# Four accumulating loads emitted earlier, and the fourth token sums split between VectorE and GpSimd

## The chip, the cores and the metric

The kernel runs on one core of one Trainium2 chip. The metric is the device time of one execution in microseconds (us). The core has five engines that run side by side, each with its own queue that it works through in order: TensorE (PE in the profile), which multiplies matrices into PSUM; VectorE (DVE) and ScalarE (ACT), which read PSUM and SBUF; GpSimd (POOL), which works on SBUF; and SyncE (SP), which only issues transfers. ScalarE and GpSimd issue some transfers as well. The data moves on 16 DMA engines that all these queues share.

## The reference

One encoder block over 1024 tokens of 1024 features, in float32. Cut to what matters:

```python
h = rms_norm(x, norm1_g)
a, gate, q, k, v = split(h @ w_in)          # 512 columns each
conv_out = conformer_conv(a, gate, ...)      # GLU, 31-tap depthwise convolution, LayerNorm, silu
attn_out = neighbourhood_attention(rms_norm(q), rms_norm(k), v, rpb)
mix = concatenate([conv_out, attn_out])      # 1024 tokens x 1024
x = x + mix @ w_out                          # output projection and residual
h = rms_norm(x, norm2_g)
x = x + (silu(h @ w_gate) * (h @ w_up)) @ w_down   # 2816 hidden features
```

The change touches two places: the residual sum `x + mix @ w_out`, and the preparation of `h` for the gate and up products.

## The kernel before

Every product of float32 matrices is made of three matmuls. An operand is split into a high part (`fp32r`, a cast by ScalarE) and the remainder (a subtraction on VectorE or GpSimd); `split` emits both, and `mac` emits the three matmuls (lines 122 to 124, 128x512 each). The cast always comes first, and the remainder waits for it.

The output projection, the gate and up products and the down product are each done as two by two blocks in seven block products in place of eight, which need sums and differences of blocks beforehand.

**The output projection** is the products n1, n7, n4, n6, n5, n2, n3, in this order. `group` (line 1112) runs one: for each of four token blocks `cb`, in the order 0, 3, 1, 2, it emits four macs and then `read`, which adds the result from PSUM into the token tiles `x2` on VectorE (`put`, line 865). n7 goes on in the PSUM of n1, and n5 in that of n6, so these reads combine two products. The `x2` tiles 0 to 3 are loaded with the rows of `x`; tiles 4 to 7 are written by the reads of n1, and the rows of `x` are added to them by a transfer that accumulates. `add_x(t)` (line 861) issues it from GpSimd's queue, 512 KB each. The reads of n5 add to tiles 0 to 3 and 4 to 7, those of n2 and n3 to 4 to 7 alone. After the last read of a tile `norm2` stores it to DRAM through SP and takes its sum of squares on ScalarE.

**What sets the order** is written out by hand. `weaves(n, s0=..., s1=...)` lays a row of n steps, and after each mac `weave()` takes one step off it: the step's instructions go into their engines' queues at that place of the program. An engine reaches them when it has done what stands before them. `take` loads and splits the next weight half (ScalarE casts, GpSimd subtracts); `QS` splits a left operand with GpSimd; `C` and `U` are transposes on TensorE with their copies on ScalarE; `N` is a normalisation on VectorE and `lo2` a remainder on VectorE. The weights' raw tiles have three buffers (`R`), so SP's next load waits until GpSimd has split an older one.

**The gate and up products.** `products` lists them: product 0 to 7 are m1 and m2 of four feature blocks, then come, in pairs of blocks 0 and 1, m6 (products 8 and 9), m5 (10 and 11), m7 (12 and 13), m3 (14 and 15) and m4 (16 and 17), and so on. Each has four macs. m6 and m5 of a block share a PSUM bank, as do m7 and m4: m5 can start only when VectorE has evacuated m6 (`u2`, line 1185). After each product `evac` takes the result out, and `prep` splits the weights of the product that comes four later (tiles `t0m`, `t1m`, ...; cast on ScalarE, remainder on GpSimd).

The left operands are sums of token blocks. `s_sum(t, 3)` makes the third sum S3 of token tile t (line 1037, into the first half of `xT`), `s_sum(t, 4)` the fourth, S4 (line 1033): two instructions of 128x256, which read `xT[t]` and `sn[t]` and write into two tiles `s4` that are taken when the first of them is emitted. `SP(name, t)` splits a sum with ScalarE and VectorE. m7 needs all four splits of S3, m3 those of S4, and m4 those of A22. A split of S4 needs the fourth sums of all four tokens. `plan` lays these steps beside the products by number: `8: dict(s1=SP("S3", 2), ...)` is emitted during product 8.

Nearly all tiles of 128x1024 come from one tag, `G`, with 22 buffers. When none is free, the first instruction that writes a new tile waits on its own engine until the last user of an older tile is done.

Of the kernel before, what the change touches and what calls it, by code (L numbers as in the profile page):

```python
# [74 lines left out]
def build(ctx, tc, a):  # L75
    nc = tc.nc
    pe, act, dve, pool = nc.tensor, nc.scalar, nc.vector, nc.gpsimd
# [560 lines left out]
    def score_mm(i):  # L638
        s_, hp = divmod(i, 4)
        rh, cb = order[s_]  # L640
        t = rh * 4 + cb
        c0, ncol, _ = WIN[cb]
        out = []
        for hh in range(2):
            s = mm(f"s{i}{hh}")[:, :AR * ncol]
            pe.matmul(s, qT[hh * HD:(hh + 1) * HD, hp, t * P:(t + 1) * P],  # L646
                      k4[hh * HD:(hh + 1) * HD, hp, rh * 4:rh * 4 + AR, c0:c0 + ncol], start=True, stop=True)
            out.append(s)
        return out
# [46 lines left out]
    rowf, diff, a11 = [], [], {}  # L696
# [45 lines left out]
    s0 = score_mm(0)  # L742
# [4 lines left out]
    s1 = score_mm(1)  # L747
# [29 lines left out]
    def q_split(n, f, j, eng):  # L777
        if j == 0:
            qop[n] = H(n, F32R)
        split(*[qop[n][:, o + j * 1024:o + j * 1024 + 1024] for o in (0, 2048)],  # L780
              f[j].rearrange("p c b q -> p (c b q)"), (eng,))
# [44 lines left out]
    def conv_silu(h, c):  # L826
        y = four(f"z{h}{c}")
        for i in range(4):
            pe.transpose(y[:, i * P:(i + 1) * P], xh[4 * h + i][:, c * P:(c + 1) * P], ident)
        act.activation(y, y, AF.Silu, bias=lnb[:, c:c + 1], scale=lng[:, c:c + 1])  # L830
        n = ("A22", "A12")[h]
        if c == 0:
            qop[n] = H(n, F32R)
        tiles = lambda w: w.rearrange("p (b i j) -> p i b j", b=4, j=16)
        hi, lo = [tiles(qop[n][:, o + c * 512:o + c * 512 + 512]) for o in (0, 2048)]
        y4 = y.rearrange("p (i b j) -> p i b j", b=4, j=16)
        split(hi, lo, y4, (dve,))
        if h == c == 0:
            tails.append(lambda: conv_diff(h, c, y4))
        else:  # L840
            conv_diff(h, c, y4)
# [10 lines left out]
    def rows(ap, t):  # L852
        rh, cb = divmod(t, 4)
        return ap.rearrange("(h i w) d -> h i w d", h=2, w=GW)[rh, :, cb * 16:cb * 16 + 16, :]
# [5 lines left out]
    def add_x(t):  # L860
        return lambda: pool.dma_start(x2[t], rows(a["x"], t), accum_op=OP.add)
# [88 lines left out]
    def norm2_out(t):  # L950
        r = SM(f"r2{t}r", 1)
        dve.reciprocal(r, sd2[t])
        xn[t] = G(f"xn{t}")
        dve.scalar_tensor_tensor(xn[t], x2[t], r, g2b, OP.mult, OP.mult)
# [68 lines left out]
    def s_sum(t, ns, eng):  # L1023
        (x11, x12), (x21, x22) = lr(xT[t]), lr(xT[t + 4])
        for n in ns:
            if n == 1:
                sn[t] = G(f"sn{t}")
            s1, s2 = lr(sn[t])
            if n == 4:
                if not s4:  # L1030
                    s4.extend(G(f"s4{j}").rearrange("p (k s) -> p k s", s=512) for j in range(2))
                for j in range(2):
                    eng.tensor_tensor(s4[j][:, :, t * P:(t + 1) * P], *[w[:, j * 256:(j + 1) * 256].rearrange(
                        "p (k s) -> p k s", s=P) for w in (x12, s2)], OP.subtract)
                continue
            o, l, r = ((s1, x21, x22), (s2, x11, s1), (x21, x11, x21))[n - 1]
            eng.tensor_tensor(o, l, r, OP.subtract)

    s4 = []
# [21 lines left out]
    def turn(t, j):  # L1061
        if not h2:
            h2.extend(H(f"h2{w}", F32R).rearrange("p (k s) -> p k s", s=512) for w in range(2))
        pt = (tp, mm)[j](f"t2{t}{j}")
        for i in range(4):
            kb = 4 * j + i
            pe.transpose(pt[:, i * P:(i + 1) * P], xn[t][:, kb * P:(kb + 1) * P], ident)
        if j == 0:
            xT[t] = G(f"xT{t}")
        w = lr(xT[t])[j]  # L1070
        if t < 4:
            hi, lo = [q[:, 4 * j:4 * j + 4, t * P:(t + 1) * P] for q in h2]
            p3 = pt.rearrange("p (k s) -> p k s", s=P)
            act.copy(hi, p3)
            act.copy(w, pt)
            rest.append(lambda: dve.tensor_tensor(lo, p3, hi.bitcast(F32), OP.subtract))
        else:
            act.copy(w, pt)
# [7 lines left out]
    def weaves(n, **at):  # L1086
        row = [[] for _ in range(n)]
        for k, fs in at.items():
            row[int(k[1:])].extend(fs if isinstance(fs, (list, tuple)) else [fs])
        woven.extend(lambda fs=fs: [f() for f in fs] for fs in row)  # L1090

    def QS(n, f, j, eng):
        return lambda: q_split(n, f, j, eng)

    def C(h, c):
        return lambda: conv_silu(h, c)

    def N(t):
        return lambda: norm2_out(t)

    def U(t, j):
        return lambda: turn(t, j)

    def SS(t, *ns, eng=dve):
        return lambda: s_sum(t, ns, eng)

    def SP(n, t, eng=dve):
        return lambda: s_split(n, t, eng)

    lo2 = lambda: rest.pop(0)()  # L1110

    def group(p, cbs=CB):
        for cb in cbs:
            more = p in ("n7", "n5")
            if not more:
                pb[cb] = mm(f"{p}{cb}")
            proj(p, cb, pb[cb], start=not more)
            read(p, cb)

    for cb in CB:  # L1120
        load_x2(cb)
    weaves(12, s0=lambda: (weigh(31), evac_hi(7), evac_lo(7)), s1=QS("Q3", diff, 0, pool), s2=lambda: tails.pop()(), s3=[lambda: read("n1", 0), add],
           s4=QS("Q3", diff, 1, pool), s6=C(0, 1), s10=take)
    group("n1", CB[1:])
    weaves(16, s1=C(0, 2), s5=take, s9=C(0, 3), s13=QS("Q2", diff, 0, pool))
    group("n7")
    weaves(16, s0=C(1, 0), s2=QS("Q2", diff, 1, pool), s4=take, s6=C(1, 1), s9=take, s12=QS("Q1", rowf, 0, pool))
    group("n4")
    weaves(16, s0=C(1, 2), s2=take, s5=C(1, 3), s7=QS("Q1", rowf, 1, pool), s10=take, s13=QS("Q4", diff, 0, pool))
    group("n6")  # L1130
    weaves(16, s1=take, s3=QS("Q4", diff, 1, pool), s6=take, s8=add_x(4), s9=N(0), s12=add_x(7), s13=N(3), s15=add_x(5))
    group("n5")
    while pos[0] < len(chunks):
        issue()
    for _ in range(3):
        next_raw()
    weaves(16, s0=take, s1=[N(1), U(0, 0)], s2=U(0, 1), s3=[lo2, lo2], s4=[U(3, 0), add_x(6)], s5=[U(3, 1), N(2)], s6=[lo2, lo2],
           s7=U(1, 0), s8=U(1, 1), s9=[lo2, lo2, prep], s10=[U(2, 0), take], s11=U(2, 1), s12=[lo2, lo2], s13=prep)
    group("n2")
    weaves(16, s3=prep, s7=prep, s9=N(4), s12=U(4, 0), s13=[U(4, 1), N(7)], s15=SS(0, 1, 2))  # L1140
# [7 lines left out]
        4: dict(s0=SP("S2", 2), s1=SP("S1", 0), s3=SP("S1", 3)),  # L1148
        5: dict(s0=SP("S1", 1), s1=SP("S1", 2), s2=SS(0, 3), s3=SS(3, 3)),
        6: dict(s0=SS(1, 3), s1=SS(2, 3), s3=SP("S3", 0)),  # L1150
        7: dict(s1=SP("S3", 3), s3=SP("S3", 1)),
        8: dict(s1=SP("S3", 2), s2=SS(0, 4, eng=pool)),
        9: dict(s0=SS(3, 4, eng=pool), s2=SS(1, 4, eng=pool)),
        10: dict(s0=SS(2, 4, eng=pool)),
        11: dict(s1=SP("S4", 0), s3=SP("S4", 1)),
        12: dict(s1=SP("S4", 2), s3=SP("S4", 3)),
        13: dict(s2=SP("A22", 0), s3=SP("A22", 1)),
# [243 lines left out]
```

## Time and profile before

| what | value |
|---|---|
| runs of the kernel, median of 3 (lowest to highest) | 1058.2 us (1057.29 to 1059.95) |
| the profiled execution's own time | 1060.61 us |
| span from its first to its last instruction | 1058.9 us |
| granted TensorE clock, mean over the span | 0.996 |
| TensorE matmuls, busy | 1033.3 us, 98% |
| VectorE, ScalarE, GpSimd busy | 68%, 44%, 43% |
| moved by DMA | 162.93 MB, 154 GB/s on the mean |

In the profile a row of the timeline gives start, duration, engine, line, operation, output and inputs, and how many instructions it merges; in brackets stand the idle time just before it and what ended it. Line 118 is the remainder and line 114 the cast of any split, so these are told apart by their tiles: `wB` is a half of B21 or B22, `wP` one of P1 to P4, `S` a token sum. `PE n` are the projection's products, `PE A`, `B` and `D` the PSUM banks of the gate and up products. A row of the stages gives the stretch, its length, each engine's busy time, the granted TensorE clock, the DMA engines' busy share and GB/s.

### The profile page before, as it was taken

The page shows a single profiled execution, that of the slowest core. Times are in us where ns is not written, and L with a number is a line of the kernel's source. Part 1 is how long each engine was busy: PE and PEld are TensorE (multiplying, and loading weights), DVE is VectorE, ACT ScalarE, POOL GpSimd, SP SyncE. Part 2 cuts the span into 40 slices and gives each one's busy share as a digit, 9 for nine tenths or more (in the row PEclk, how much of TensorE's full clock was granted, in tenths as well). Part 3 has the DMA queues.
Part 4 walks back from the last instruction along what each step waited for, and adds up shares of the span by engine and source line. Part 5 has one row for each costly group of instructions (what it writes and reads, how often), then busy time and mean ns, then how long its engine had stood idle before and what let it go on. Part 6 is the DMA issues. An engine that isn't in the chain of part 4 may idle for free.

```text
span 1058.9 us, 13907 instructions
## 1 busy us (share of the span) xinstructions
PE 1033.3 (98%) x4972; PEld 836.4 (79%) x4972; DVE 721.1 (68%) x1093; ACT 465.4 (44%) x915; POOL 455.8 (43%) x346
## 2 busy tenths in 40 slices
PE   7999999999999998999999999999999999999997
PEld 6888888776658877778888888888888888888885
DVE  6768999966895464867564564655646567758883
ACT  6455346627776556642323323232232444433441
POOL 0236668923575753675554445544455200002310
PEclk9999999999999999999999999999999999999999
DMA  9595872285545285355322233232231597633641
GB/s 337 180 260 196 236 241 78 70 238 172 151 107 163 83 213 161 100 140 183 125 100 90 110 113 112 75 129 100 83 136 73 192 328 264 208 100 121 216 132 40
DMA packets 74677, 162.93 MB, mean 154 GB/s; under 512 B 13488, under 2 KB 22192, under 8 KB 73904
## 3 DMA queue, kind: packets, MB, share of 16 engines
q1 hardware_dynamic: 67776, 144.14, 39.8%
q0 software_dynamic: 4864, 10.49, 5.9%
q10 hardware_dynamic: 1968, 7.42, 2.1%
q8 instruction: 39, 0.64, 0.2%
q14 instruction: 30, 0.25, 0.1%
HBM read 122.86 MB, written 53.15 MB: 166 GB/s over the span
## 4 chain that ended last, share of the span: by engine, by line
PE 55%; DVE 1%; issue 0%; POOL 0%; ACT 0%; DVEq 0%
PE B L123 5%; PE B L122 5%; PE B L124 5%; PE D L123 4%; PE D L124 4%; PE D L122 4%; PE A L123 3%; PE A L122 3%; PE A L124 3%; PE B2d L122 1%; PE B2d L123 1%; PE B2d L124 1%; PE A3d L122 1%; PE A2d L122 1%; PE A1d L122 1%; PE A0d L122 1%
## 5 line engine op out<-in xcount | busy, mean ns | idle before, releaser
L347 DVE SCALAR_TENSOR_TENSOR cv<-u,par,cv 128x1009 f32<-128x1009 f32 (+14 forms) x85 | 108.5, 1276 | 1.9
L373 POOL TENSOR_TENSOR pa<-pa,pr 128x1022 f32<-128x1022 f32 (+10 forms) x31 | 75.2, 2427 | 32.2 <-ACT pr L372 31.4
L1356 POOL TENSOR_TENSOR ou<-ou,resm 128x512 f32<-128x512 f32 x8 | 12.4, 1545 | 142.4 <-DMA resm<-xd 141.8
L114 ACT CAST op<-sr 128x512 fp32r<-128x512 f32 x77 | 47.6, 619 | 52.1 <-PE B2d L124 22.2
L118 DVE TENSOR_TENSOR op<-sr,op 128x512 fp32r<-128x512 f32 x77 | 59.2, 769 | 14.7 <-ACT op L114 14.7
L1193 DVE TENSOR_TENSOR g<-B,g 128x512 f32<-128x512 f32 x22 | 15.2, 690 | 74.0 <-PE B L124 74.0
L1202 ACT ACTIVATE D<-D 128x512 f32<-128x512 f32 x22 | 12.8, 582 | 113.3 <-DVE D L1201 113.3
L1185 DVE TENSOR_TENSOR u<-B,g 128x512 f32<-128x512 f32 x22 | 15.1, 690 | 61.1 <-PE B L124 61.1
L668 POOL TENSOR_SCALAR e<-e,rs 128x288 f32<-128x288 f32 (+1 forms) x64 | 34.9, 567 | 45.6 <-DVE rs L666 41.0
L114 ACT CAST op<-wd 128x512 fp32r<-128x512 f32 x66 | 40.9, 620 | 31.0 <-DVE wd L1280 17.1
L118 DVE TENSOR_TENSOR op<-wd,op 128x512 fp32r<-128x512 f32 x66 | 50.4, 764 | 2.6 <-ACT op L114 1.1
L986 DVE TENSOR_TENSOR ts<-ts,gu 128x512 f32<-128x512 f32 x36 | 43.3, 1202 | 0.6
L1191 ACT ACTIVATE A<-A 128x512 f32<-128x512 f32 x18 | 10.5, 582 | 68.6 <-PE A L124 68.6
L661 ACT ACTIVATE e<-e,mx 128x288 f32<-128x288 f32 (+1 forms) x64 | 36.2, 569 | 3.0 <-DVE mx L659 3.0
L865 DVE TENSOR_TENSOR x<-x,n 128x512 f32<-128x512 f32 x32 | 21.0, 681 | 22.7 <-PE n L124 14.3
L659 DVE CUSTOM_DVE_ANT_0 e<-s,tab 128x288 f32<-128x288 f32 (+1 forms) x64 | 29.7, 500 | 8.7 <-PE s L646 8.4
L372 ACT ACTIVATE pr<-u,par 128x1022 f32<-128x1022 f32 (+10 forms) x31 | 34.2, 1135 | 1.2 <-ACT vs L433 1.2
L677 PEld LDWEIGHTS p<-ident,e 128*96 128x96 f32 (+1 forms) x192 | 20.0, 133 | 18.0 <-POOL e L668 10.4
L677 PE MATMUL p<-ident,e 128*96 128x128 f32 (+1 forms) x192 | 28.5, 281 | 2.3 <-DVE pT L682 1.0
L986 DVE TENSOR_TENSOR ts<-gu 128x512 f32<-128x512 f32 x18 | 30.1, 1670 | 0.0
L693 PE MATMUL o<-pT,vw 96*64 96x128 f32 (+1 forms) x384 | 28.0, 281 | 0.0
L646 PE MATMUL s<-kT,qT 64*128 64x288 f32 (+1 forms) x128 | 26.7, 495 | 0.0
(1065 smaller groups left out, 3525.9 us busy)
## 6 DMA issues: line engine op xcount, KB each, us to landing
sr<-sd SPq DMA_DIRECT2D x77, 256.0 KB
gu<-in_gu SPq DMA_DIRECT2D x36, 512.0 KB
sd<-sd SPq DMA_DIRECT2D x22, 512.0 KB
wd<-in_wd SPq DMA_DIRECT2D x44, 256.0 KB
sd<-g SPq DMA_DIRECT2D x33, 256.0 KB
x<-in_x SPq DMA_DIRECT2D x12, 512.0 KB
xd<-x SPq DMA_DIRECT2D x8, 512.0 KB
resm<-xd SPq DMA_DIRECT2D x16, 256.0 KB
```

The source lines that it names most:

```text
L114: act.copy(hi, src)
L118: eng.tensor_tensor(*[w[..., sl] for w in (lo, src, hi.bitcast(F32))], OP.subtract)
L122: pe.matmul(acc, lh, rh, start=start, stop=False, skip_group_check=True)
L123: pe.matmul(acc, lh, rl, start=False, stop=False, skip_group_check=True)
L124: pe.matmul(acc, ll, rh, start=False, stop=stop, skip_group_check=True)
L347: dve.scalar_tensor_tensor(acc[:, o], uc[:, i], dwk[:, c, t:t + 1], acc[:, o], OP.mult, OP.add)
L372: act.activation(pr[:, o], uc[:, i], AF.Copy, scale=dwk[:, c, t:t + 1])
L373: pool.tensor_tensor(pa[:, o], pa[:, o], pr[:, o], OP.add)
L661: act.activation(e[:, hh], e[:, hh], AF.Exp, bias=mx, scale=-1.0, accum_out=rs[:, hh:hh + 1])
L668: pool.tensor_scalar(es[i][:, hh], es[i][:, hh], rs[:, hh:hh + 1], 1.0, op0=OP.mult, op1=OP.mult)
L677: pe.transpose(pt[:m, g * P:(g + 1) * P], es[i][:, hh, g * m:(g + 1) * m], ident)
L986: dve.tensor_tensor(lr(tsum[i, 1])[n - 3] if o is None else o, l, r, OP.add)
```

## The change

Four steps `add_x` are taken out of the rows of n5 and n2 and put into those of n7, n4 and n6. Token tiles 4 to 7 thus receive the rows of `x` before the reads of n5 add to them; before the change they received them between the reads of n5 and those of n2.

In `plan`, the fourth sums of tokens 0 and 3 stay on GpSimd and move one product earlier; those of tokens 1 and 2 go to VectorE, into products 9 and 10. The splits of S3 for tokens 1 and 2 move from products 7 and 8 to 9 and 10, in front of those sums.

```diff
     group("n1", CB[1:])
-    weaves(16, s1=C(0, 2), s5=take, s9=C(0, 3), s13=QS("Q2", diff, 0, pool))
+    weaves(16, s1=C(0, 2), s5=take, s9=C(0, 3), s11=add_x(4), s13=QS("Q2", diff, 0, pool))
     group("n7")
-    weaves(16, s0=C(1, 0), s2=QS("Q2", diff, 1, pool), s4=take, s6=C(1, 1), s9=take, s12=QS("Q1", rowf, 0, pool))
+    weaves(16, s0=C(1, 0), s1=add_x(7), s2=QS("Q2", diff, 1, pool), s4=take, s6=C(1, 1), s8=add_x(5), s9=take, s12=QS("Q1", rowf, 0, pool))
     group("n4")
-    weaves(16, s0=C(1, 2), s2=take, s5=C(1, 3), s7=QS("Q1", rowf, 1, pool), s10=take, s13=QS("Q4", diff, 0, pool))
+    weaves(16, s0=C(1, 2), s1=add_x(6), s2=take, s5=C(1, 3), s7=QS("Q1", rowf, 1, pool), s10=take, s13=QS("Q4", diff, 0, pool))
     group("n6")
-    weaves(16, s1=take, s3=QS("Q4", diff, 1, pool), s6=take, s8=add_x(4), s9=N(0), s12=add_x(7), s13=N(3), s15=add_x(5))
+    weaves(16, s1=take, s3=QS("Q4", diff, 1, pool), s6=take, s9=N(0), s13=N(3))
     group("n5")
...
-    weaves(16, s0=take, s1=[N(1), U(0, 0)], s2=U(0, 1), s3=[lo2, lo2], s4=[U(3, 0), add_x(6)], s5=[U(3, 1), N(2)], s6=[lo2, lo2],
+    weaves(16, s0=take, s1=[N(1), U(0, 0)], s2=U(0, 1), s3=[lo2, lo2], s4=U(3, 0), s5=[U(3, 1), N(2)], s6=[lo2, lo2],
            s7=U(1, 0), s8=U(1, 1), s9=[lo2, lo2, prep], s10=[U(2, 0), take], s11=U(2, 1), s12=[lo2, lo2], s13=prep)
     group("n2")
...
         6: dict(s0=SS(1, 3), s1=SS(2, 3), s3=SP("S3", 0)),
-        7: dict(s1=SP("S3", 3), s3=SP("S3", 1)),
-        8: dict(s1=SP("S3", 2), s2=SS(0, 4, eng=pool)),
-        9: dict(s0=SS(3, 4, eng=pool), s2=SS(1, 4, eng=pool)),
-        10: dict(s0=SS(2, 4, eng=pool)),
+        7: dict(s1=SP("S3", 3), s2=SS(0, 4, eng=pool)),
+        8: dict(s2=SS(3, 4, eng=pool)),
+        9: dict(s1=SP("S3", 1), s3=SS(1, 4)),
+        10: dict(s1=SP("S3", 2), s3=SS(2, 4)),
         11: dict(s1=SP("S4", 0), s3=SP("S4", 1)),
```

## The prediction

> **What bounds the kernel now.** I read the page first: TensorE (PE) is busy for 98% of the span, so the edit can only give back time that PE loses. I then asked for PE's waits.
>
> ```profile
> PE 1033.3 (98%) x4972; PEld 836.4 (79%) x4972; DVE 721.1 (68%) x1093; ACT 465.4 (44%) x915; POOL 455.8 (43%) x346
> ```
> ```profile
> PE t L1067 <- DVE x L865: 2.6, 1, 2.6
> ...
> PE B L123 <- DVE S L118: 1.5, 2, 0.7
> ...
> PE n L122 <- ACT wB L114: 0.8, 1, 0.8
> ```
>
> Of the list (engine, what it waited for, us in total, times, longest), these three are a read of the projection, a token split and a weight cast. Apart from one at the start, all the long waits lie between 388 and 463 us, in the code that the diff touches. PE's timeline shows what each costs, halved clock included.
>
> ```profile
> 379.61 0.39 PE L122 MATMUL n<-wB,A 128*128 128x512 f32 x1
> 380.29 0.39 PE L122 MATMUL n<-wB,A 128*128 128x512 f32 x1
> ...
> 381.33 0.48 PE L122 MATMUL n<-wB,A 128*128 128x512 f32 x1
> ...
> 382.46 0.48 PE L122 MATMUL n<-wB,A 128*128 128x512 f32 x1
> ...
> 390.75 1.12 PE L1067 MATMUL t<-ident,xn 128*128 128x128 f32 x4 [2.56 <-DVE x L865]
> ...
> 398.47 0.39 PE L122 MATMUL n<-wB,Q 128*128 128x512 f32 x1
> ...
> 403.26 0.50 PE L123 MATMUL n<-wB,Q 128*128 128x512 f32 x1 [1.95 <-POOL wB L118]
> ...
> 415.25 0.39 PE L122 MATMUL A<-h,t0m 128*128 128x512 f32 x1
> ```
>
> A mac (three matmuls) is 0.68 us, 379.61 to 380.29; a mac with a transpose group is 1.13, 381.33 to 382.46, so a group is 0.45. Product n2 has 16 macs and 8 groups: 10.9 + 3.6 = 14.5, but took 398.47 - 379.61 = 18.9. Stall A costs **4.4**. Product n3 has 16 macs and 2 groups, 11.8, but took 415.25 - 398.47 = 16.8. Stall B costs **5.0**. More than half of each is idling; most of the rest is a halved clock just after it:
>
> ```profile
> 392.00:394.00 2.00, 2.00 (x6) 1.52 (x5) 1.29 (x3) 0.98 (x2) 0.00 (x0) 0.50 1.04 270
> ```
>
> Further on, in the gate and up products:
>
> ```profile
> 440.13 0.39 PE L122 MATMUL B<-S,t0m 128*128 128x512 f32 x1
> ...
> 447.12 0.47 PE L122 MATMUL B<-S,t0m 128*128 128x512 f32 x1 [1.39 <-DVE u L1185]
> ...
> 458.11 0.39 PE L122 MATMUL B<-S,t0m 128*128 128x512 f32 x1
> ...
> 463.13 0.39 PE L122 MATMUL B<-S,t1m 128*128 128x512 f32 x1
> ...
> 469.28 0.39 PE L122 MATMUL D<-A,t1m 128*128 128x512 f32 x1
> ```
>
> These rows start products 8, 10, 14, 15 and 17, each of four macs, 2.72. Product 10 is 6.99 - 5.44 = **1.55** late (stall C); 14 takes 5.02 and 15 with 16 takes 6.15, so 2.3 + 0.7 = **3.0** more (stall D). All four together are 13.9 us.
>
> **Part 1, the four adding transfers.** What stalls A and B hang on:
>
> ```profile
> 390.01 0.69 DVE L865 TENSOR_TENSOR x<-x,n 128x512 f32<-128x512 f32 x1 [3.51 <-DMA x<-in_x]
> ```
> ```profile
> 381.83 3.37 SPq L977 DMA_DIRECT2D gu0None<-in_gu  x1
> ```
> ```profile
> 398.23 0.62 ACT L114 CAST t0m<-gu0None 128x512 fp32r<-128x512 f32 x1 [5.25 <-DMA gu0None<-in_gu]
> ```
> ```profile
> 379.65 2.99 POOL L861 DMA_DIRECT2D x<-in_x  x3
> ```
> ```profile
> DMA to landing us min/median/max: 10.3/15.1/18.9
> ```
> ```profile
> 350.00:355.00 5.00, 5.00 (x25) 4.14 (x25) 2.52 (x4) 3.23 (x4) 5.00 (x3) 1.00 0.08 24
> 355.00:360.00 5.00, 5.00 (x26) 4.13 (x25) 1.13 (x3) 1.77 (x3) 3.23 (x2) 1.00 0.54 186
> ...
> 375.00:380.00 5.00, 5.00 (x24) 4.14 (x23) 4.93 (x8) 3.86 (x8) 5.00 (x3) 1.00 1.01 339
> ...
> 385.00:390.00 5.00, 3.19 (x19) 2.33 (x16) 1.27 (x2) 3.69 (x8) 2.21 (x2) 1.00 1.03 207
> ```
>
> Stall A: the read of n2 into token tile 4 waits until 390.01 for its add, issued after 379.65. That read frees the PSUM bank that the next transposes want. Moved to n7, n4 and n6, the adds are issued some 20 to 35 us sooner, where the DMA engines are 8 to 54% busy; even the longest landing, 18.9, is in time. The read then follows VectorE's program order and ends near 387.1, before PE wants the bank at 388.0. **A goes: -4.4** (bounds 0 and -4.4).
>
> Stall B: ScalarE sits 5.25 us on the first gate weights; behind that cast, in its order, stands the cast of the last half of B22, and GpSimd's split of it ends at 403.26. From 398.23 that is 5.0 us. Unstalled, n3 begins at 394.1 and wants this half 1.6 later, so the weights must land by 390.7. With the adds' 2.1 MB gone, the last store (0.5 MB) and the weights (0.5 MB) need 1.5 us each at the 339 GB/s at which the stores went alone: near 386 if SP's issue is no longer held for 3.37, 398.2 if the adds are not what holds it. I take the former, as the rate falls from 339 to 207 with the adds. **B goes: -5.0** (bounds 0 and -5.0).
>
> What it costs: each issue holds GpSimd about 1.0 us (2.99 for 3). GpSimd's queue where they go, and SP's:
>
> ```profile
> 348.75 2.40 POOL L118 TENSOR_TENSOR Q<-df,Q 128x1024 fp32r<-128x1024 f32 x1 [2.82 <-ACT Q L114]
> ...
> 353.48 2.40 POOL L118 TENSOR_TENSOR wP<-P21r,wP 128x1024 fp32r<-128x1024 f32 x1
> ...
> 360.60 2.39 POOL L118 TENSOR_TENSOR wP<-P10r,wP 128x1024 fp32r<-128x1024 f32 x1 [2.37 <-ACT wP L114]
> ```
> ```profile
> 353.55 0.32 SPq L157 DMA_DIRECT2D P11r<-w4P  x1
> ```
>
> Two fall before the gap of 2.82 or in it, the third pushes the second half of P2 and a Q1 split by 1.0, and the gap of 2.37 takes that and the fourth. P2's half then ends near 356.9. PE wants it in the third mac of n6, at 358.5: n2's start less two products of 10.9 and two groups is 356.8, and 1.6 on. **Cost 0**; without the gaps 4 x 1.0. The adds also come into the DMA engines beside the SP loads of P1 and B21. P1's second half, asked for at 353.55, is wanted in n5 at 370.3 (368.7 and 1.6): cost 0 again, and rival 5 if not.
>
> **Part 2, the token sums and splits.** VectorE before, with ScalarE and GpSimd behind it:
>
> ```profile
> 422.49 0.69 DVE L118 TENSOR_TENSOR S<-sn,S 128x512 fp32r<-128x512 f32 x1 [2.45 <-ACT S L114]
> ...
> 441.15 5.22 DVE L118 TENSOR_TENSOR S<-xT,S 128x512 fp32r<-128x512 f32 x4
> 446.30 1.28 DVE L1185 TENSOR_TENSOR u<-B,g 128x512 f32<-128x512 f32 x2
> ...
> 455.58 3.52 DVE L118 TENSOR_TENSOR S<-s,S 128x512 fp32r<-128x512 f32 x2 [4.74 <-ACT S L114]
> ...
> 465.32 1.28 DVE L118 TENSOR_TENSOR A<-xT,A 128x512 fp32r<-128x512 f32 x2
> ```
> ```profile
> 441.16 1.83 POOL L118 TENSOR_TENSOR t0m<-gum,t0m 128x512 fp32r<-128x512 f32 x1 [2.29 <-ACT t0m L114]
> ```
> ```profile
> 446.99 0.62 ACT L114 CAST t0m<-gum 128x512 fp32r<-128x512 f32 x1 [3.35 <-POOL s L1033]
> ```
> ```profile
> L1033 POOL TENSOR_TENSOR s<-xT,sn x8: 731/910/1180, 444.6 to 454.5; 128x256 f32<-128x256 f32 x8
> L118 DVE TENSOR_TENSOR S<-s,S x4: 1180/1779/1810, 455.6 to 460.7; 128x512 fp32r<-128x512 f32 x4
> ```
>
> Stall C is four splits of S3 ahead of product 8's evacuation. Two of them move behind it: it starts near 443.7, product 10 is on time, C goes. But product 9's evacuation now has in front of it the split S3 1 and token 1's fourth sum. When can S3 1 start? Its cast on ScalarE stands behind the casts of two weight blocks, t1m for product 11 and t0m for product 12. The row at 446.99 shows such a cast waiting for a fourth sum that it doesn't read: what it needs is a buffer. All 22 G buffers are in use, and the sum's inputs are the next to be freed. With the first sum one product earlier, and its two output tiles too, I put that release at 445.1: GpSimd is free at 443.0, and a sum is two instructions of 0.73 to 1.18. Then t1m, t0m and S3 1 are cast, 0.62 each, and VectorE has S3 1 at 447.0: one split (0.69 alone, 1.81 at most), then two half sums. VectorE showed none of these; nearest is half a 128x512 operation, 0.35, and in turns with GpSimd's 0.73 about 1.1. I take 0.69 and 1.1 each, as GpSimd has sums and splits waiting. The evacuation starts near 449.9 and product 11 at 450.6, wanted at 448.3 (440.13 and three products): **a new stall of 2.3** (0 with a free buffer and no turns; 3.1 if the buffer comes only when product 9 ends, as before).
>
> Stall D is S4 late: GpSimd ends its eight half sums after 454.5 and S4's first split starts at 455.58. After, the last sum is VectorE's, near 452.2, and the splits start near 452.9. From 455.58 the S4 and A22 splits took until 466.6 (465.32 and 1.28), 11.0 us; so they end near 463.9, and product 16, 2.3 late itself, wants them at 464.4 (440.13, eight products, one matmul and the 2.3). **D goes**, by 0.5 only. So C and D turn from 4.55 into 2.3.
>
> Does the new stall halve the clock? The stalls with 2.56 and with 0.83 and 1.95 us of idling did, the one with 1.39 did not; 2.1 idle falls between. A halved stretch costs 1.7 (3.4 us at 0.50). The odds are about even and I charge **0.85**.
>
> By the Trainium skill (TensorE: Matmul & The Clock Gate, "Why this matters for your kernels") the clock drops only after a gap of about 3 us or more. The row at 390.75 speaks against that, since 2.56 us were enough. By that rule the sum would be 0.85 better.
>
> The Trainium skill (SBUF — State Buffer, "SBUF: two separate sides") says that VectorE with two SBUF inputs and GpSimd hold a shared port by turns, each for a whole instruction. It is a rule against handing VectorE sums beside GpSimd; the 1779 ns row against 0.69 alone agrees.
>
> **Sum:** -4.4 - 5.0 + (2.3 + 0.85 - 4.55 = -1.4) = -10.8. The profiled execution took 1060.6 (span 1058.9 and 1.7 around it) and would take 1049.8. The median of the runs, 1058.2, is 2.4 lower: **1047.5**.
>
> **The rivals.**
> 1. No new stall: a buffer is free in time. The 13.9 go whole: 1044.3. For it, the wait is about a buffer alone; against it, 22 buffers were all taken at 446.99.
> 2. The gate weights stay late because the stores fill the queues. B stays: 1052.4. For it, the DMA share is 1.01 with stores alone; against it, those stores run at 339.
> 3. The buffer comes only when product 9 ends: a stall of 3.1 and a halved clock, 4.8 in place of 4.55: 1049.1. For it, the first sum had to wait just so before; against it, the sums ask before the casts do now.
> 4. No halving at 2.1 us of idling: 1046.7. For it, 1.39 us of idling did nothing; against it, 2.56 did.
> 5. The early adds starve P1's second half as they did the gate weights. With the longest landing, 18.9, it is there at 372.4, its cast (half the 2.4 of a split) and split end at 376.0, against 370.3: 5.7 and a halved clock, 7.4. Then 1054.9, about no change to be seen. Against it, the DMA is 8 to 54% busy there.
> 6. Slower: VectorE becomes the bound in products 8 to 17. If each of the 16 splits and sums from 441.15 is held by GpSimd for the full 1.81, with seven evacuations of 0.64 (half of 1.28), that is 33.4 and ends at 474.6; without a new stall product 16 wants it at 462.1. That is 12.5, and three halved stretches, 5.1: 17.6. It decides from 13.9 on, and 17.6 - 13.9 gives 1061.9. For it, the 1.81 row; against it, four S3 splits took 5.22, not 7.2.
>
> **How the numbers follow.** Forecast 0.42, rivals in order 0.13, 0.10, 0.13, 0.10, 0.06, 0.06. The forecast's own range is 1046.7 to 1048.4 (the clock). Holding all but 2 in 10 takes rivals 1 to 4: 1044 to 1052.5. About 0.3%, 3.2 us, is what can be told from no change; so faster (under 1055.0) is 0.88, same 0.06, slower 0.06.
>
> **What would show it.** After the change VectorE's reads in n2 wait for no DMA and n2 takes near 14.5; the cast of the first gate weights waits for none and n3 takes near 11.8; PE's clock is 1.00 from 380 to 405. The S4 wait before 455.58 is gone. A new PE wait of about 2 us for the evacuation stands at product 11, and S3 1's cast waits behind one for a buffer. The prediction is wrong if n2 or n3 keep their length, if product 11 starts on time, or if a new wait on a weight split shows in n6 or n5.

## The result, and the profile after

| | before | after |
|---|---|---|
| median of 5 runs each, one chip | 1058.2 us | **1050.37 us** |
| lowest to highest | 1057.29 to 1059.95 | 1049.88 to 1051.02 |
| the profiled execution's own time | 1060.61 | 1050.14 |
| its span | 1058.9 | 1048.4 |

The ratio is 0.9923, with a 95% interval from 0.9908 to 0.9937. The change is faster by 7.8 us. The forecast was 1047.5, so 2.9 us were expected that did not come; the range, 1044.0 to 1052.5, holds the time, the forecast's own range up to 1048.4 does not.

First TensorE's waits after the change (engine, what it waited for, us in total, times, longest):

```profile
PE z L122 <- ACT wk0h L114: 7.3, 1, 7.3
PE B L122 <- DVE u L1185: 1.4, 1, 1.4
...
PE D L123 <- DVE A L118: 0.4, 1, 0.4
PE B L123 <- DVE S L118: 0.3, 1, 0.3
```

The read of `x` and the cast and split of `wB`, stalls A and B, are gone from the list. The wait for `u` at line 1185 is there with nearly the same length, but it is another one: it now stands at product 11, whose timeline row follows. The wait at the start, for `wk0h`, is 0.9 longer than before and no part of the change.

TensorE's timeline after, with the starts of n2, n3, the first gate product, product 8, product 10, product 11 and product 18 (the first behind the pairs that the change touches):

```profile
380.01 0.39 PE L122 MATMUL n<-wB,A 128*128 128x512 f32 x1
...
394.57 0.39 PE L122 MATMUL n<-wB,Q 128*128 128x512 f32 x1
...
406.38 0.39 PE L122 MATMUL A<-h,t0m 128*128 128x512 f32 x1
...
431.26 0.39 PE L122 MATMUL B<-S,t0m 128*128 128x512 f32 x1
...
436.70 0.39 PE L122 MATMUL B<-S,t0m 128*128 128x512 f32 x1
...
441.03 0.47 PE L122 MATMUL B<-S,t1m 128*128 128x512 f32 x1 [1.45 <-DVE u L1185]
...
461.47 0.39 PE L122 MATMUL B<-S,t2m 128*128 128x512 f32 x1
```

| stretch | before | forecast | after |
|---|---|---|---|
| n2 | 18.86 | 14.5 | 14.56 |
| n3 | 16.78 | 11.8 | 11.81 |
| products 0 to 7 | 24.88 | 24.88 | 24.88 |
| products 8 to 17 (10 x 2.72 = 27.2 without a wait) | 31.87 | 27.2 + 2.3 + 0.85 = 30.35 | 30.21 |
| sum | 92.39 | 81.5 | 81.46 |

So this stretch came out as forecast, to 0.1 us, and the miss must lie elsewhere. (In the row of products 8 to 17 that is luck: its two losses are not the forecast ones, as shown below.) The rest of the profiled execution, own time less this sum, was 1060.61 - 92.39 = 968.2 before and 1050.14 - 81.46 = 968.7 after.

The stages by time, of before and then of after (stretch, its length, busy time of PE, PEld, DVE, ACT and POOL with counts, granted clock, DMA share, GB/s):

```profile
380.00:400.00 20.00, 17.43 (x85) 13.87 (x84) 9.87 (x16) 10.08 (x20) 6.94 (x6) 0.91 0.94 198
400.00:420.00 20.00, 17.23 (x78) 13.88 (x78) 12.09 (x18) 11.51 (x24) 6.39 (x5) 0.91 0.56 189
```
```profile
380.00:400.00 20.00, 20.00 (x105) 16.66 (x104) 13.30 (x20) 14.62 (x28) 8.66 (x6) 1.00 0.43 144
400.00:420.00 20.00, 20.00 (x105) 16.66 (x104) 13.78 (x19) 14.59 (x29) 5.01 (x4) 1.00 0.43 148
```

TensorE has no gap left in these 40 us, the clock is 1.00 throughout, and the DMA share in the first half has fallen from 0.94 to 0.43. The first gate weights in the view of their tile, after the change (duration in ns: least, median, most; first and last start):

```profile
L114 ACT CAST t0m<-gu0None x2: 632/642/651, 390.0 to 394.3; 128x512 fp32r<-128x512 f32 x2
...
L977 SPq DMA_DIRECT2D gu0None<-in_gu x1: 377/377/377, 382.2 to 382.2; - x1
```

SP's issue takes 0.38 us and not 3.37, and the cast runs at 390.0 without a wait for the transfer, where it began at 398.23 before.

The new stall at product 11 on ScalarE and VectorE:

```profile
436.00 0.62 ACT L114 CAST t1m<-gum 128x512 fp32r<-128x512 f32 x1 [2.75 <-POOL s L1033]
436.53 0.62 ACT L114 CAST t0m<-gum 128x512 fp32r<-128x512 f32 x1
437.05 0.62 ACT L114 CAST S<-xT 128x512 fp32r<-128x512 f32 x1
```
```profile
437.69 0.84 DVE L118 TENSOR_TENSOR S<-xT,S 128x512 fp32r<-128x512 f32 x1 [2.42 <-ACT S L114]
438.46 1.83 DVE L1033 TENSOR_TENSOR s<-xT,sn 128x256 f32<-128x256 f32 x2
440.21 0.68 DVE L1185 TENSOR_TENSOR u<-B,g 128x512 f32<-128x512 f32 x1
```

Two casts of weight blocks, released by a fourth sum that they don't read, then S3 1's cast; then S3 1's split, two half sums, and the evacuation that product 11 wants. That is the forecast's chain, link by link. Product 11 starts at 441.03; on time it would start one product after product 10, at 436.70 + 2.72 = 439.42. It is 1.61 late (2.3 forecast). The other 30.21 - 27.2 - 1.61 = **1.40** is lost at products 14 to 17, where the forecast had nothing. There VectorE's longest single row, then its last splits of A22, and GpSimd beside the first:

```profile
443.16 4.54 DVE L118 TENSOR_TENSOR S<-s,S 128x512 fp32r<-128x512 f32 x1
```
```profile
454.79 1.28 DVE L118 TENSOR_TENSOR A<-xT,A 128x512 fp32r<-128x512 f32 x2
```
```profile
442.92 1.74 POOL L118 TENSOR_TENSOR t1m<-gum,t1m 128x512 fp32r<-128x512 f32 x1
444.18 1.73 POOL L118 TENSOR_TENSOR t0m<-gum,t0m 128x512 fp32r<-128x512 f32 x1
445.42 1.73 POOL L118 TENSOR_TENSOR t1m<-gum,t1m 128x512 fp32r<-128x512 f32 x1
```

A split of S4 that takes 0.68 alone took 4.54. It ends at 447.70, 0.55 after the third of three weight splits that GpSimd ran one behind the other (445.42 + 1.73), and the last split of A22 ends at 456.07.

### The profile page after: what moved, and what is told of

It reads as the page before. It is cut to its first block, busy times and chain, and to the rows that moved or that the text cites. A ratio compares the mean times of both kernels' runs of the same rounds, so it can differ in the third digit from the quotient of the medians.

```text
span 1048.4 us, 13903 instructions
## 1 busy us (share of the span) xinstructions
PE 1028.2 (98%) x4972; PEld 833.8 (80%) x4972; DVE 722.9 (69%) x1097; ACT 465.3 (44%) x915; POOL 452.6 (43%) x342
## 4 chain that ended last, share of the span: by engine, by line
PE 88%; DVE 4%; POOL 2%; DMA 2%; ACT 2%; issue 2%; SPq 0%; POOLq 0%; ACTq 0%; DVEq 0%
PE B L122 5%; PE B L123 5%; PE B L124 5%; PE D L123 4%; PE D L124 4%; PE D L122 4%; PE A L122 3%; PE A L123 3%; PE A L124 3%; PE z L123 3%; PE z L122 3%; PE z L124 3%; PE gl L124 3%; PE gl L123 3%; PE gl L122 3%; PE n L122 3%
```

## The experiments

Three questions: what each part of the change is worth; where the 2.9 us went that the forecast had too much; and whether the two losses left at products 11 and 14 to 17 have the causes that the traces suggest. My theory for the second, formed on the result: the profiled execution of before was longer than the median by something inside the stalls that the change removes, so it could not be subtracted once more. Its rival: a profile adds a constant to this kernel.

All kernels are read by the same four starts on TensorE's timeline (n2, n3, product 8, product 18) of their profiled execution. "Lost" is product 18 less product 8, less 27.2; "stretch" is product 18 less n2; "rest" is that execution's own time less the stretch. The kernel before is shown by its own two profiles.

| kernel | n2 | n3 | p8 | p18 | lost | stretch | own time | rest |
|---|---|---|---|---|---|---|---|---|
| before | 379.61 | 398.47 | 440.13 | 472.00 | 4.67 | 92.39 | 1060.61 | 968.2 |
| before, second profile | 379.43 | 399.62 | 438.14 | 470.02 | 4.68 | 90.59 | 1058.59 | 968.0 |
| after | 380.01 | 394.57 | 431.26 | 461.47 | 3.01 | 81.46 | 1050.14 | 968.7 |
| after, second profile | 379.51 | 394.08 | 430.77 | 461.70 | 3.73 | 82.19 | 1050.22 | 968.0 |
| adds alone | 379.64 | 394.20 | 430.89 | 462.79 | 4.70 | 83.15 | 1051.12 | 968.0 |
| plan alone | 379.08 | 398.42 | 439.81 | 470.62 | 3.61 | 91.54 | 1059.19 | 967.7 |
| one add alone | 378.93 | 393.49 | 438.26 | 470.13 | 4.67 | 91.20 | 1058.62 | 967.4 |
| after, no adds | 379.98 | 394.54 | 431.21 | 461.87 | 3.46 | 81.89 | 1050.38 | 968.5 |
| sums on GpSimd | 380.26 | 394.82 | 431.49 | 463.42 | 4.73 | 83.16 | 1051.96 | 968.8 |
| early casts | 380.15 | 394.71 | 431.37 | 461.83 | 3.26 | 81.68 | 1050.37 | 968.7 |
| one weight split moved | 379.66 | 394.24 | 430.92 | 460.86 | 2.74 | 81.20 | 1049.30 | 968.1 |
| casts and weight split | 379.39 | 393.96 | 430.65 | 459.74 | 1.89 | 80.35 | 1048.21 | 967.9 |
| the same, second profile | 379.90 | 394.46 | 431.15 | 460.65 | 2.30 | 80.75 | 1049.15 | 968.4 |
| and A22 sooner | 379.43 | 393.99 | 430.68 | 458.17 | 0.29 | 78.74 | 1047.08 | 968.3 |

The rest stays between 967.4 and 968.8 in all fourteen, while the stretch goes from 92.4 to 78.7. So what these kernels gain and lose does lie in this stretch, up to 0.7 us either way. Two profiles of one kernel differ by up to 0.7 in "lost", so smaller differences in that column say nothing by themselves.

### Each part alone

**The adds alone**: the first half of the diff, with the old plan.

```diff
-        7: dict(s1=SP("S3", 3), s2=SS(0, 4, eng=pool)),
...
+        7: dict(s1=SP("S3", 3), s3=SP("S3", 1)),
...
```

> The four adding transfers moved as in the change, the token sums as before. Theory 1 (the transfers hold stalls A and B, 9.4 us with their halved clock; the sums are worth 1.6, since in the changed kernel's trace stalls C and D went from 4.55 to 2.9): n2 takes 14.6 and n3 11.8, no halved clock, stalls C and D stay at about 4.5, and the median is 1.6 above the changed kernel's 1050.4, 1052.0. Rival (the median fell by 2.9 less than I forecast because the transfers gain less without the profiler): 1053.5 or more.

Measured 1051.12 (1050.97 to 1051.39), beside 1058.38 before on that chip: ratio 0.9934, 0.9921 to 0.9946. So the adds are worth 7.3 us of the medians, and C and D stay (4.70 lost).

**The plan alone**: the second half of the diff, with the adds at their old places.

```diff
-        7: dict(s1=SP("S3", 3), s3=SP("S3", 1)),
-        8: dict(s1=SP("S3", 2), s2=SS(0, 4, eng=pool)),
-        9: dict(s0=SS(3, 4, eng=pool), s2=SS(1, 4, eng=pool)),
-        10: dict(s0=SS(2, 4, eng=pool)),
+        7: dict(s1=SP("S3", 3), s2=SS(0, 4, eng=pool)),
+        8: dict(s2=SS(3, 4, eng=pool)),
+        9: dict(s1=SP("S3", 1), s3=SS(1, 4)),
+        10: dict(s1=SP("S3", 2), s3=SS(2, 4)),
```

> The token sums and splits as in the change, the adding transfers as before. Theory 1: stalls A and B stay with their halved clock, product 11 waits about 1.6 and D costs about 1.3; the median is 1.6 below before's, 1056.6. Rival (the sums lose time when the profiler is off): 1058.2 or above.

Measured 1057.72 (1055.94 to 1059.29), ratio 0.9991, 0.9982 to 1.0. By time alone that is not told apart from nothing. In the trace 3.61 are lost in place of 4.67: some 1 us is gained, of the 1.4 forecast.

**The changed kernel without the four adds.**

```diff
-s11=add_x(4),
...
-s1=add_x(7),
...
-s8=add_x(5),
...
-s1=add_x(6),
```

> The changed kernel without the four adding transfers, so the rows of x are missing from half of the residual; it leaves that addition out. It prices the early transfers. Theory 1 (they cost nothing where they are now): the same as the changed kernel within 0.7 us, 1050.4, and GpSimd's splits between 345 and 365 us are shorter. Rival (the early transfers, whose issues hold GpSimd for 1.0 to 2.0 each and share the DMA engines, cost part of the missing gain): 1048 or less.

Measured 1050.55 (1050.29 to 1051.18), as after. At their new places the adds cost nothing, as the forecast had it.

### Stalls A and B: one add alone

Only the add of token tile 4 moves, the one that the read behind stall A waits for.

```diff
-    weaves(16, s1=C(0, 2), s5=take, s9=C(0, 3), s13=QS("Q2", diff, 0, pool))
+    weaves(16, s1=C(0, 2), s5=take, s9=C(0, 3), s11=add_x(4), s13=QS("Q2", diff, 0, pool))
...
-    weaves(16, s1=take, s3=QS("Q4", diff, 1, pool), s6=take, s8=add_x(4), s9=N(0), s12=add_x(7), s13=N(3), s15=add_x(5))
+    weaves(16, s1=take, s3=QS("Q4", diff, 1, pool), s6=take, s9=N(0), s12=add_x(7), s13=N(3), s15=add_x(5))
```

> Only the transfer for token tile 4 is early, as in the change; those for 7, 5 and 6 stay where they were, and so do the sums. It tells stall A (the read that waits for tile 4) from stall B (the late gate weights). Theory 1: the read of tile 4 waits for no transfer, but the reads of tiles 7 or 5 may; the first gate weights still land late, near 396, because three adds are still in flight, so the cast of the last half of B22 still holds n3: n3 keeps more than 14 of its 16.8 us. Median about 1054.5. Rival (stall B follows from stall A, a chain that begins with tile 4): both go, about 1050 to 1052.

Measured 1059.24 (1057.35 to 1060.32), ratio 1.0003, 0.9994 to 1.0012. A miss: nothing is gained. n2 takes 393.49 - 378.93 = 14.56, so A is gone; but n3 now takes 19.88 (its next start is 413.37) and not 16.78. Its waits and the gate weights' tile:

```profile
PE n L122 <- ACT wB L114: 2.7, 1, 2.7
PE n L123 <- POOL wB L118: 1.9, 1, 1.9
```
```profile
400.16 0.79 PE L123 MATMUL n<-wB,Q 128*128 128x512 f32 x1 [1.94 <-POOL wB L118]
```
```profile
L114 ACT CAST t0m<-gu0None x2: 617/632/648, 395.1 to 399.0; 128x512 fp32r<-128x512 f32 x2
...
L977 SPq DMA_DIRECT2D gu0None<-in_gu x1: 3279/3279/3279, 381.1 to 381.1; - x1
```

Stall B ends when the gate weights have landed and been cast, whenever n3 begins. With two adds in flight and a third to come SP's issue still takes 3.28, and the cast begins at 395.1, 3.1 sooner than before. Counted from the start of n2, n3 begins 4.3 sooner, but its last wait ends only 2.4 sooner (400.16 - 378.93 = 21.23 beside 403.26 - 379.61 = 23.65): B's wait takes back 1.9 of what A gives. The clock takes half of the rest or, beside the second profile of before (below), all of it. It is halved for 6.8 us here (0.87, 0.50, 0.50, 0.50 and 0.92 in the five 2 us stages from 398 to 408), and from the end of that wait to the first gate product it takes 13.21 us, where it took 11.99 in the first profile of before, with 3.4 us halved behind this wait, and 10.36 in the second, with none. In sum n2 and n3 take 34.44, beside 35.64 and 33.83. So A and B are not two terms to be added. That A alone is worth nothing is measured; how it divides between wait and clock is read from one execution. Only when the weights come early (390.0 after the change) do both stalls go.

### Where the 2.9 us went: before, profiled once more

No edit.

> The kernel before, once more with a profile. Its unprofiled times lie in two groups about 1.9 us apart (1057.5 to 1058.5 and 1059.3 to 1060.7), about what one stretch of 3.41 us at half clock costs (1.7). Theory (which stalls are followed by a halved stretch differs from execution to execution, since the stalls' idling is near what halves the clock): a profiled execution of the lower group, if one is caught, has its PE products in the same places up to the stalls and one halved stretch fewer (one of the 380 to 410 windows at 1.00), and the profiled times differ by about 1.7 for it. Rival (profiling adds a constant 2.4 to this kernel): the profiled execution takes 1060.6 again with the clock at 0.91 in both windows.

This execution took 1058.59, at the lower group's upper end. Its TensorE waits on the timeline, and two stages of it; behind them stages of the first profile of before:

```profile
390.46 0.66 PE L1067 MATMUL t<-ident,xn 128*128 128x128 f32 x4 [2.46 <-DVE x L865]
...
396.73 0.50 PE L122 MATMUL n<-wB,A 128*128 128x512 f32 x1 [2.50 <-DVE x L865]
...
402.90 0.50 PE L123 MATMUL n<-wB,Q 128*128 128x512 f32 x1 [1.53 <-POOL wB L118]
```
```profile
390.00:394.00 4.00, 3.54 (x21) 2.81 (x21) 2.96 (x5) 1.08 (x2) 0.00 (x0) 1.00 1.05 262
404.00:408.00 4.00, 4.00 (x19) 3.31 (x18) 2.09 (x5) 2.15 (x5) 1.84 (x3) 1.00 0.77 206
```
```profile
390.00:392.00 2.00, 1.25 (x5) 1.25 (x6) 1.96 (x3) 0.09 (x1) 0.00 (x0) 0.66 0.95 217
...
404.00:406.00 2.00, 2.00 (x7) 1.52 (x7) 0.69 (x1) 0.34 (x1) 1.68 (x2) 0.58 0.72 262
406.00:408.00 2.00, 2.00 (x7) 1.56 (x6) 0.00 (x0) 1.61 (x4) 0.28 (x1) 0.57 0.61 150
```

The same program, with stalls at the same transfers (here two reads of n2 wait, for 2.46 and 2.50), and in the second profile the clock is 1.00 in both places where the first had it halved. Its n2 and n3 together take 33.83 and not 35.64, which is 1.8 of the 2.0 us between the two own times; the rest is alike (968.0 and 968.2). It is only 1.8, though two halved stretches of 1.7 each are missing: the first of them passes in the time that n2 and n3 wait for the adds and the weights anyway (n2 is even longer here, 20.2, and n3 3.1 shorter).

So the theory holds and the constant does not: what the first profile had above the median lay in halved clock behind the stalls. The scatter agrees: on one chip the 21 runs of before went from 1057.51 to 1060.73, the five with the adds alone from 1050.97 to 1051.39; the eleven each with the plan alone and with one add alone, which keep stalls, are spread over 3.4 and 3.0 us.

### Product 11 and the sums

**Fourth sums on GpSimd**, the changed kernel otherwise:

```diff
-        9: dict(s1=SP("S3", 1), s3=SS(1, 4)),
-        10: dict(s1=SP("S3", 2), s3=SS(2, 4)),
+        9: dict(s1=SP("S3", 1), s3=SS(1, 4, eng=pool)),
+        10: dict(s1=SP("S3", 2), s3=SS(2, 4, eng=pool)),
```

> The changed kernel, but with the fourth sums of tokens 1 and 2 back on GpSimd (all four sums there), in the same products 9 and 10 as VectorE has them after the change; S3's splits stay apart. Tells what VectorE's sums cost or save by themselves. Theory (the stall at product 11 is the wait for the cast, 2.42, plus the two sums' 1.83 ahead of the evacuation): without the sums the evacuation follows S3 1's split at 438.5 and product 11 is on time, -1.6; but the sums then queue behind GpSimd's weight splits, S4 is late as before (3.0 lost rather than 1.3), +1.7: near 1050.4, with the loss at products 14 to 17. Rival (the sums on VectorE are what gains in the plan): product 11 gains nothing and the time is 1052.

Measured 1051.38 (1051.13 to 1051.96), between the two, nearer to neither's reasons: product 11 is on time (439.65 after 436.93), as the theory had it, but 4.73 are lost, as much as before the change. The time went to S4:

```profile
447.01 3.50 DVE L118 TENSOR_TENSOR S<-s,S 128x512 fp32r<-128x512 f32 x2 [3.84 <-ACT S L114]
```
```profile
445.17 1.85 POOL L1033 TENSOR_TENSOR s<-xT,sn 128x256 f32<-128x256 f32 x2
446.56 1.70 POOL L118 TENSOR_TENSOR t0m<-gum,t0m 128x512 fp32r<-128x512 f32 x1
```

GpSimd reaches the last sum at 445.17, and S4's first split starts at 447.01, 3.85 later than after the change. So moving S3's splits apart gains nothing by itself: it carries the loss from product 10 to product 14. What the plan gains, it gains by VectorE's sums.

**Early casts**: ScalarE's casts of S3 1 and S3 2 are emitted in products 7 and 8, ahead of the weight casts that wait for a buffer. VectorE's part stays where it is.

The helpers `SC` (the cast alone) and `SR` (the remainder alone), which `SP` emits together, are not shown:

```diff
...
-        7: dict(s1=SP("S3", 3), s2=SS(0, 4, eng=pool)),
-        8: dict(s2=SS(3, 4, eng=pool)),
-        9: dict(s1=SP("S3", 1), s3=SS(1, 4)),
-        10: dict(s1=SP("S3", 2), s3=SS(2, 4)),
+        7: dict(s1=[SP("S3", 3), SC("S3", 1)], s2=SS(0, 4, eng=pool)),
+        8: dict(s1=SC("S3", 2), s2=SS(3, 4, eng=pool)),
+        9: dict(s1=SR("S3", 1), s3=SS(1, 4)),
+        10: dict(s1=SR("S3", 2), s3=SS(2, 4)),
```

> After the change, product 11 starts 1.61 us late: the cast of S3 1 on ScalarE stands behind the casts of t1m and t0m, which wait 2.75 us for a G buffer, and VectorE's split, two half sums and the evacuation of product 9 stand behind it. Here the casts of S3 1 and S3 2 are emitted two products sooner (products 7 and 8), ahead of those weight casts; VectorE's remainders stay in products 9 and 10. Theory (the cast's place behind the waiting weight cast makes the stall): VectorE's split is ready near 436, its sums and the evacuation end before 439.4, product 11 is on time, the S4 splits come sooner, and the time falls by 1.6 to 2.9, to 1047.5 to 1048.8. Rival (VectorE is simply full, and held by GpSimd): product 11 stays late and the time stays at 1050.4.

Measured 1050.54 (1049.64 to 1051.14): the rival's time, but not its reason. Product 11 starts at 439.53, on time, so the cast's place was the cause of that stall. The loss has moved once more, to products 14 to 17:

```profile
442.46 5.83 DVE L118 TENSOR_TENSOR S<-s,S 128x512 fp32r<-128x512 f32 x2 [0.91 <-ACT S L114]
```
```profile
443.51 1.73 POOL L118 TENSOR_TENSOR t1m<-gum,t1m 128x512 fp32r<-128x512 f32 x1
444.77 1.72 POOL L118 TENSOR_TENSOR t0m<-gum,t0m 128x512 fp32r<-128x512 f32 x1
446.02 1.70 POOL L118 TENSOR_TENSOR t1m<-gum,t1m 128x512 fp32r<-128x512 f32 x1
```

S4's first two splits end at 448.29, no sooner than after the change (448.30), though VectorE came to them at 442.46 and not 443.16. Three GpSimd splits stand one behind the other there too.

### The split that is held

**One weight split moved**: the remainder of the block for product 14, the middle one of the three, goes to VectorE, ahead of S4. First in the changed kernel, then in the one with early casts.

```diff
-            split(*top[i, p], src, (pool,))
+            split(*top[i, p], src, (dve if n_prep[1] == 15 else pool,))
```

> The changed kernel with the same one weight split moved from GpSimd to VectorE, and nothing else. Product 11's stall of 1.61 has nothing to do with that split and should stay; S4's split of 4.54 us should fall under 2.5, and products 14 to 17 lose under 0.5 instead of 1.3. Theory (held over back-to-back GpSimd instructions): 1049.3 to 1049.8. Rival (VectorE is full): 1050.4 or up to 1.8 more.

> The kernel with the early casts of S3 1 and S3 2, and in it one weight split (the remainder of the t0m block for product 14) moved from GpSimd to VectorE, ahead of S4's first split there. In the kernel with the early casts, product 11 was on time, but S4's first two splits took 5.83 us on VectorE (0.68 each alone) while GpSimd ran three weight splits back to back, and products 14 to 17 lost 3.2 us instead of 1.3. Theory (VectorE gets no turn between GpSimd's instructions when they follow each other without a gap): with the middle one of the three gone from GpSimd and ahead of S4 on VectorE, the first two S4 splits end near 446 and not 448.3, products 14 to 17 lose under 1, and the time is 1047.5 to 1048.5. Rival (VectorE itself is full in products 8 to 17, so that a split more there costs its own length): 1050.5 or up to 1.8 more.

In the changed kernel 1049.74 (1049.30 to 1050.08), with early casts 1048.60 (1048.09 to 1050.94), both beside 1058.9: ratios 0.9911 (0.9896 to 0.9926) and 0.9908 (0.9891 to 0.9924). The times fall into the theory's bounds or within 0.1 of them, and against the rival VectorE was not full: it took on a split and the time did not rise. The losses at products 14 to 17 were larger than expected, though: 2.74 less the 1.63 at product 11 is 1.1 (under 0.5), and 1.89 (under 1). And in the changed kernel it was the moved split that was now held, over GpSimd's two:

```profile
442.85 3.29 DVE L118 TENSOR_TENSOR t0m<-gum,t0m 128x512 fp32r<-128x512 f32 x1
```
```profile
442.60 2.97 POOL L118 TENSOR_TENSOR t1m<-gum,t1m 128x512 fp32r<-128x512 f32 x2
```

3.29 in place of the 0.72 that it took with early casts, where it came before GpSimd's pair; it ends at 446.14, 0.57 after the pair. S4's two splits behind it then take 1.28 and are done at 447.34, where they were done at 448.30 before the move. Products 14 to 16 start on time in both, and what is left there is lost at product 17, whose start waits for the splits of A22 that product 16 wants.

**A22's splits sooner**, on top of both, so that they fall into the gap that GpSimd has around 447:

```diff
-        12: dict(s1=SP("S4", 2), s3=SP("S4", 3)),
-        13: dict(s2=SP("A22", 0), s3=SP("A22", 1)),
-        14: dict(s1=SP("A22", 2), s3=SP("A22", 3)),
+        12: dict(s1=SP("S4", 2), s3=[SP("S4", 3), SP("A22", 0), SP("A22", 1)]),
+        13: dict(s2=SP("A22", 2), s3=SP("A22", 3)),
```

It ran on one chip with the changed kernel and with the one before this step.

> The kernel with the early casts and the weight split on VectorE, in which the only loss left in this stretch is 1.84 at product 17 (product 16 waits 1.5 in its first mac for A22's last splits: two A22 splits took 3.07 beside GpSimd's weight splits, and their casts stood behind one that waited 4.03 for a transfer). Here A22's splits come one product sooner, so that the first two casts stand ahead of that one and the splits fall into a gap of 2.66 on GpSimd. Theory: product 16's wait goes, 1.5 to 1.8 less, near 1047.0. Rival (the evacuations of products 12 and 13, now behind these splits on VectorE, turn late instead): 1048.6 or more.

> The kernel with the early casts and one weight split on VectorE, once more, beside the changed kernel on one chip. Theory: 1048.6, 1.8 below the changed kernel. Rival (its gain is of the chip that it ran on): 1050.4.

> The changed kernel, unaltered, on the same chip as the run with A22's splits sooner and the repeat of the one before it, for a comparison without a change of chip. Expected 1050.4, with both others below it. If the three agree within 0.5, the gains seen in their traces are not there in the times.

| one chip | median | lowest to highest | ratio to before (1060.0) |
|---|---|---|---|
| changed kernel | 1050.22 | 1049.65 to 1050.84 | 0.9905 (0.9889 to 0.9921) |
| casts and weight split | 1048.66 | 1048.31 to 1049.15 | 0.989 (0.9872 to 0.9908) |
| and A22 sooner | **1047.09** | 1046.20 to 1047.73 | 0.9875 (0.9856 to 0.9893) |

The three don't overlap, and each step is what was forecast for it. The last on VectorE, and TensorE's longest waits in it:

```profile
448.07 1.28 DVE L118 TENSOR_TENSOR A<-xT,A 128x512 fp32r<-128x512 f32 x2
449.27 0.68 DVE L1212 TENSOR_TENSOR g<-g,D 128x512 f32<-128x512 f32 x1
449.87 2.89 DVE L118 TENSOR_TENSOR A<-xT,A 128x512 fp32r<-128x512 f32 x2
```
```profile
PE z L122 <- ACT wk0h L114: 6.2, 1, 6.2
PE p L677 <- DVE pT L682: 1.0, 2, 0.6
```

A22's first two splits run unheld (1.28), and none of the waits between n2 and product 17 is among the longest any more: 0.29 are lost. This version beats the changed kernel by 3.1 us.

## Why the prediction was right, and where it failed

**Right, stalls A and B.** n2 14.56 and n3 11.81 (14.5 and 11.8); no read waits for a transfer, the first gate cast neither; the cause, that the adds in flight hold SP's issue and the weights, shows in 3.37, 3.28 and 0.38 us with four, three and none of the adds at their old places. Not right is that A and B stood as two terms, -4.4 and -5.0: A by itself is worth nothing in the median, and in its trace a longer wait in B and a halved clock behind it take most of what it gives.

**Right, the adds' cost of 0**: the kernel without any add is as fast, and no wait on P1's or P2's halves turned up (rival 5).

**Right in kind, the new stall at product 11**: the same casts in the same order, and it went when S3 1's cast was put ahead of them. Mis-sized, 2.3 for 1.61. Product 8 starts 8.87 sooner than before, so VectorE had S3 1 at 437.69 + 8.87 = 446.6 in the old clock (447.0 forecast), and the two sums took 1.83 (1.1 each). The 0.85 for a halved clock was not due either: the clock stayed at 1.00, as rival 4 had it.

**Wrong, "D goes".** 1.40 is lost at products 14 to 17 (2.1 in the second profile). The step that failed is the 11.0 us for the S4 and A22 splits, taken over from before as one block, and behind it "1.81 at most": the forecast let no VectorE split be held for longer. In the first profile the splits begin at 443.16, 0.9 sooner than forecast (452.9 less 8.87 is 444.0), and end at 456.07 (454.79 and 1.28, the last A22 row), so they take 12.9; most of the difference is the one split held for 4.54. In the second profile another instruction is held, the second half of token 2's fourth sum, just ahead of S4:

```profile
441.75 5.08 DVE L1033 TENSOR_TENSOR s<-xT,sn 128x256 f32<-128x256 f32 x1
```

There S4's splits begin only at 447.36, and with A22's they take 8.9. So what is held varies, and the block of 11.0 holds in neither. The trace of before already had a VectorE instruction held for more than twice 1.81, behind the stretch that the forecast looked at, while GpSimd issued a transfer and then ran three weight splits until 484.79:

```profile
480.97 4.38 DVE L1227 TENSOR_TENSOR sd<-sd,g 128x512 f32<-128x512 f32 x1
```
```profile
479.78 1.20 POOL L1001 DMA_DIRECT2D gum<-in_g  x1 [3.11 <-DVE sd L1227]
```

The stall of 2.3 + 0.85 and D's 0 came to 3.15, the two losses to 3.01: the sum was right by errors that cancel, and in the second profile, with 3.73, by 0.6 less so.

**Wrong, the last step: "The median of the runs, 1058.2, is 2.4 lower: 1047.5".** The forecast for the profiled execution, 1049.8, was right (1050.14, and n2 started 0.4 later, which the kernel's second profile does not show). Then 2.4 was taken off once more, as if the profiled execution's surplus were in the part that stays. By the two profiles of before it was in the part that goes: halved clock behind A and B, which differs from execution to execution. A median run of before had less to lose. By the second profile (stretch 90.59) the change takes 90.6 - 81.5 = 9.1 off 1058.6, which is 1049.5; most of what is left to 1050.37 is the rest, 968.7 and not 968.0. From a sum for the length after, 968.2 + 81.5 = 1049.7, no knowledge of before's scatter would have been needed.

**The rivals.** No new stall (1) and weights that stay late (2) didn't come, nor a buffer only at product 9's end (3). VectorE as the bound (6) didn't come as a whole: VectorE took a further split at a gain. But its means, a VectorE instruction held by GpSimd, was the one that cost D its gain, and for longer than its 1.81.

## What to carry to other kernels

Where the runs of the kernel before scatter, first find out whether its profiled execution's surplus lies in what the change removes: then add up the length after, and don't subtract the gain from the median. A stall that stands ahead of a wait for a transfer is not a term of its own: taking it away can lengthen that wait, and a halved clock behind the wait can take the rest. And a VectorE operation with two SBUF inputs belongs into a gap of GpSimd, not beside a run of its instructions, least of all, as far as these traces go, one that begins with a transfer issue; product 11's stall was taken away in two ways here, and both times the loss came back at products 14 to 17, until one weight split had left GpSimd and A22's splits lay in such a gap.

## What the runs showed of the hardware that was not expected

**VectorE held over several GpSimd instructions.** The forecast let VectorE have its turn after each. Held over three weight splits a 0.68 us split took 4.54, over two 3.29, and it ended 0.55 and 0.57 after the last. In the kernel with the sums on GpSimd, though, two S4 splits beside weight splits without a gap took 3.50, 1.75 each, so there they did have turns. One thing that the traces show sets these cases apart. GpSimd's run after the change begins with its issue of a transfer (line 1001), and the held split starts during that issue, at 443.16:

```profile
442.12 1.21 POOL L1001 DMA_DIRECT2D gum<-in_g  x1 [0.70 <-DVE S L118]
```

It is so in all fourteen profiles: between 425 and 486 us VectorE has 46 instructions of more than 1.9 us, and each starts during such an issue or at most 0.14 us after its end; those that came to a later split of a run took 1.9 at most. With the sums on GpSimd the issue ended at 444.33 (443.12 and 1.21), and S4's splits came at 447.01. No run here moves the issue alone, so whether it is the cause stays open. The Trainium skill (SBUF — State Buffer, "Who interferes with whom") says that issue order decides who is blocked, and that a VectorE instruction with two SBUF inputs contends with one of GpSimd that reads SBUF. The rows agree with the second. With the first they agree only for the first of the three weight splits, which began at 442.92, before VectorE's split; the other two, from 444.18 and 445.42, began after it and went first as well. That the wait can go on over a whole run of instructions stands in none of its sentences.

**The same stall halves the clock in one execution and not in the next.** After 2.56 us of idling it was halved, after 2.46 and 2.50 in the second profile it was not. From the rows of the first profile, 0.66 of the stage from 390 is a halving from 390.64 on, 0.58 of that from 404 one from 404.32 on: 13.7 us apart, and the first lasts 3.4 (1.36, 2.00 and 0.08 of three stages). 13.7 is four times 3.4, and the 6.8 us in the run with one add are twice 3.4. The Trainium skill (TensorE: Matmul & The Clock Gate, "Part 1: The HAM clock gate (the "warmup" mystery)") says that activity is counted in windows of 3.4 us that run freely, so that the outcome depends on where the work falls in them. These rows agree, and the forecast's even odds by the length of the idling alone were the wrong question. That the second profile's stalls fell across two windows is inferred; no run shows it.
